# Normed input rows split once, column sums and forget gate in groups of 32 columns, and an opening whose order is written out for all engines

## The chip, the cores and the metric

The kernel runs on one core of one Trainium2 chip. The metric is the device time of one execution in microseconds (us). Engine names are those of the profile: PE (matrix multiply), PEld (its weight loads), DVE (vector), ACT (activation functions), POOL (general purpose), SP (the queue that issues most transfers).

## What is computed

One layer of a trunk over 528 tokens (16 learned ones and 512 of the input), width 1024. The input is normed by the root of the mean of its squares, one large projection gives the features of two branches and their gates, both branches are merged, and a wide MLP follows. Cut to what the change touches:

```python
u = rmsnorm(h, norm_mix[l])                 # u = h * g * rsqrt(mean(h*h) + eps)
proj = u @ w_in[l]
...
f = f + mu * (token_shift(f) - f)
r, k, v, wd, ad, gd = jnp.split(f, ...)
w_log = -jax.nn.softplus(-(w0 + jnp.tanh(wd) @ w_lora_up)) - DECAY_OFFSET
g = jax.nn.sigmoid(gd) @ g_lora_up
...
log_f = jax.nn.log_sigmoid(fl.astype(jnp.float32) + b_f)    # forget gate, 8 heads
F = jnp.cumsum(log_f, axis=1)
```

## The kernel before

All matrices lie with features on the 128 partitions and tokens along the free axis. The 528 tokens are held in two halves of 264 (t = 0 and 1), the 1024 features in eight blocks k of 128 rows, loaded as four chunks c of two blocks each (tiles `xt0` and `xt1`, rows transposed on the host). A product in fp32 accuracy is made of three passes over operands that are split in a high part and a rest, both of type fp32r: high weight with high input, high weight with input rest, weight rest with high input. A split costs ACT a cast (the high part) and DVE a subtraction (the rest). The input's parts are `uhi` and `ulo`, a weight block's are `whi` and `wlo`, made from the loaded `wraw`.

The **opening** works on the two halves one after the other. For each chunk ACT squares it (L352), and PE adds the squares over the partitions with a 128x128 matrix of ones in plain fp32 (L360). At the same time the rows, times the gain of the norm but not yet divided by the root, are split (ACT L355, DVE L356), so that PE can go on at once with the forget gate's eight columns (L365, 24 matmuls of 8 output rows for each half) and with the first weight block, LORA (L304, 24 matmuls for each half). ACT makes the root as an exponential of a logarithm (L368, L369), and DVE multiplies it into the products (L377). The forget gate's logarithm and its running sum follow here (L381 to L387). PE then takes the second weight block, GD, for both halves, while DVE multiplies gain and root into the rows in place (L398) and ACT and DVE split these normed rows a second time (L400, L401). All later projections read this second split.

The results of LORA and GD go through the token shift (`tshift`: ACT L317, DVE L318), a tanh, and another split into `lhi` and `llo` (L270, L271).

After the opening a **planner** sets the order on PE. Streams of work are generators that yield a time at which they can go on; the class `Turns` picks by rank the first stream that is ready by a clock model (`Clock`), whose costs are constants in the code. The streams are: `recurrent` (for each of four pairs of heads: `decay`, `keys`, `rows`, `scores`, `bonus`), `attention`, `fox_features`, `projections` (the weight blocks, L501, 48 matmuls each, which fill PE in between), and later the `chain` streams. The other engines' order is set by the framework's scheduler from priorities. In this kernel the planner's clock starts after the opening (`ck = Clock(nc)` ahead of `turns = Turns(tc, ck)`).

The first pair's work after the opening, in the order in which each step feeds the next: `decay` takes 12 small matmuls `pup` (L733) of `lhi` and `llo`, ACT's tanh (L255) to `sg` and `tha`, a scan on DVE to `lc` (L738), exponentials on ACT to `P` and `lc` (L740, L741). `keys` takes the projected `okk`, squares it (ACT L750), sums per head on PE (`pkk`, L754), takes a logarithm and an exponential on ACT (L757, L758), scales `okk` (DVE L761), and makes `KT` and `BK` on DVE and POOL (L766 to L772). `rows` makes `L` from `okk`, `P` and the second projected block `orr` (DVE L778, L781; ACT L780, L782). `scores` is three times 12 small matmuls `psr` (L807) and three transposes `pbt` (L814), with DVE reading the former out (`Bm`, L808, and `L`, L810). Weight blocks that these steps need are `okk`, `orr` and `ov` (columns `B_PAIR + 3` to `B_PAIR + 5` of the first pair), then the attention's.

All transfers of the opening are issued on SP's queue in program order: parameters, the four chunks of `xt0`, LORA's weights, `xt1`, GD's weights, constants.

## Time and profile before

| | |
|---|---|
| Median of three runs | 848.72 us (846.47 to 850.33) |
| The profiled execution: its own time, its span | 849.18 us, 847.4 us |
| PE busy in the span | 825.8 us (97%) |
| DVE, ACT, POOL busy | 616.5, 454.2, 135.1 us |
| First matmul starts | 4.89 us |
| Last matmul of the opening's two blocks (L304) starts | about 32.0 us |
| Third group of transposes `pbt` starts | 65.14 us |

The profile is of one execution. Its times count from the start of the span, which is 1.8 us shorter than that execution's own time. Engines work at the same time; a busy share says how much of a stretch an engine worked, and the waits say for whom it stood still. Matmuls are pipelined, so one that the profile gives as 0.28 us long is followed by the next after less than half of that; where the text speaks of a step, it means the time from the start of one instruction to the start of the next of a row of equal ones.

### The profile page before, as it was taken

To read this page: it belongs to the slowest core of one execution; us is meant where nothing else is said; L and a number is where in the kernel's file an instruction comes from. 1 tells how busy PE (TensorE), PEld (TensorE's weight loads), DVE (VectorE), ACT (ScalarE), POOL (GpSimd) and SP (SyncE) were. 2 spreads that over 40 slices of the span, in tenths; PEclk is the share of its full clock that TensorE was granted. 3 is DMA by queue.
4 is the path that set the end of the run, shared out by engine and by line. 5 is a ranking of instruction groups with operands and counts; after the bars stand their busy time and mean duration, and the time that the engine had idled before them with its cause. 6 is when DMAs were issued, how large, how long until landed. Compare 5 with 4: busy or idle time off the path is not lost.

```text
span 847.4 us, 15278 instructions
## 1 busy us (share of the span) xinstructions
PE 825.8 (97%) x5740; PEld 678.1 (80%) x5740; DVE 616.5 (73%) x1222; ACT 454.2 (54%) x923; POOL 135.1 (16%) x133
## 2 busy tenths in 40 slices
PE   7889999999999999999999999999999999999998
PEld 6878987878887787677788779888888888888886
DVE  6996996679867965665457564876777677768688
ACT  7767536765656337644555452665355435544452
POOL 1041300004012000000022001203700560055000
PEclk9999999999999999999999999999999999999999
DMA  6231231110222212123486422651743274245421
GB/s 229 58 103 58 72 113 43 45 59 26 77 88 87 75 52 89 51 75 113 138 272 218 154 88 82 201 153 51 248 149 100 85 244 132 86 136 189 119 92 74
DMA packets 51338, 95.88 MB, mean 113 GB/s; under 512 B 5816, under 2 KB 6968, under 8 KB 51264
## 3 DMA queue, kind: packets, MB, share of 16 engines
q1 hardware_dynamic: 47680, 86.52, 32.1%
q0 software_dynamic: 1280, 4.20, 1.6%
q10 hardware_dynamic: 2304, 4.20, 1.5%
q8 instruction: 45, 0.74, 0.4%
q14 instruction: 29, 0.24, 0.1%
HBM read 88.57 MB, written 6.31 MB: 112 GB/s over the span
## 4 chain that ended last, share of the span: by engine, by line
PE 80%; DVE 5%; DMA 4%; ACT 4%; issue 2%; POOL 1%; SPq 0%; ACTq 0%; DVEq 0%; POOLq 0%
PE pj L501 25%; PE po L1150 21%; PE po L1268 12%; PE pd L1268 5%; DMA gl<-gd 2%; PE pw L858 2%; PE po L1120 2%; PE psc L611 1%; DMA wraw<-in_wo 1%; PE py L656 1%; PE ppt L640 1%; PE psr L807 1%; PE pssq L553 1%; PE pch L918 1%; PE pch L924 1%
## 5 line engine op out<-in xcount | busy, mean ns | idle before, releaser
L501 PE MATMUL pj<-uhi,whi 128*128 128x264 f32 (+1 forms) x480 | 165.7, 345 | 0.0
L501 PE MATMUL pj<-ulo,whi 128*128 128x264 f32 (+1 forms) x480 | 154.2, 321 | 1.6 <-DVE ulo L401 1.6
L501 PE MATMUL pj<-uhi,wlo 128*128 128x264 f32 (+1 forms) x480 | 154.0, 321 | 0.0
L501 PEld LDWEIGHTS pj<-uhi,whi 128*128 128x128 f32 x480 | 90.2, 188 | 15.0 <-issue 6.7
L501 PEld LDWEIGHTS pj<-ulo,whi 128*128 128x128 f32 x480 | 90.5, 188 | 8.6 <-DVE ulo L401 2.0
L501 PEld LDWEIGHTS pj<-uhi,wlo 128*128 128x128 f32 x480 | 90.3, 188 | 6.9
L236 DVE TENSOR_TENSOR wlo<-wraw,whi 128x512 fp32r<-128x512 f32 x88 | 68.2, 785 | 37.9 <-ACT whi L235 35.6
L1150 PE MATMUL po<-zhi,whi 128*128 128x512 f32 (+1 forms) x248 | 94.8, 382 | 0.0
L1150 PE MATMUL po<-zlo,whi 128*128 128x512 f32 (+1 forms) x248 | 94.8, 382 | 0.0
L1150 PE MATMUL po<-zhi,wlo 128*128 128x512 f32 (+1 forms) x248 | 94.8, 382 | 0.0
L235 ACT CAST whi<-wraw 128x512 fp32r<-128x512 f32 x88 | 53.7, 616 | 51.5 <-DMA wraw<-in_wup 19.3
L471 DVE TENSOR_TENSOR wlo<-wraw,whi 128x512 fp32r<-128x512 f32 x80 | 61.9, 781 | 17.5 <-ACT whi L470 17.0
L470 ACT CAST whi<-wraw 128x512 fp32r<-128x512 f32 x80 | 49.1, 618 | 43.8 <-PE pj L501 43.2
L270 ACT CAST whi<-t 128x512 fp32r<-128x512 f32 x64 | 39.9, 623 | 44.4 <-DVE wlo L271 20.6
L271 DVE TENSOR_TENSOR wlo<-t,whi 128x512 fp32r<-128x512 f32 x64 | 49.4, 784 | 18.8 <-ACT whi L270 18.0
L1268 PE MATMUL po<-wlo,fhi 128*128 128x512 f32 x160 | 62.7, 392 | 0.2 <-DVE wlo L271 0.2
L1268 PE MATMUL po<-whi,flo 128*128 128x512 f32 x160 | 62.3, 390 | 0.0
L1268 PE MATMUL po<-whi,fhi 128*128 128x512 f32 x160 | 62.0, 389 | 0.0
L1196 POOL TENSOR_TENSOR t<-traw 128x512 f32<-128x512 f32 x24 | 35.3, 1475 | 154.0 <-DVE wlo L271 135.8
L1150 PEld LDWEIGHTS po<-zhi,wlo 128*128 128x128 f32 x248 | 46.6, 188 | 9.0
L1150 PEld LDWEIGHTS po<-zhi,whi 128*128 128x128 f32 x248 | 46.6, 188 | 9.0
L1150 PEld LDWEIGHTS po<-zlo,whi 128*128 128x128 f32 x248 | 46.6, 188 | 9.0
(307 smaller groups left out, 1758.5 us busy)
## 6 DMA issues: line engine op xcount, KB each, us to landing
wraw<-in_win SPq DMA_DIRECT2D x84, 256.0 KB, 2.6
wraw<-in_wup SPq DMA_DIRECT2D x64, 256.0 KB, 3.4
wraw<-in_wdn SPq DMA_DIRECT2D x48, 256.0 KB, 2.6
traw<-in_wdn SPq DMA_DIRECT2D x48, 256.0 KB, 3.1
gd<-gt ACTq DMA_DIRECT2D x16, 256.0 KB, 2.3
wraw<-in_wout SPq DMA_DIRECT2D x16, 256.0 KB, 2.9
gl<-gd SPq DMA_DIRECT2D x16, 256.0 KB, 3.5
wraw<-in_wo SPq DMA_DIRECT2D x16, 256.0 KB, 3.3
```

What stands on the lines that cost most here:

```text
L235: A.copy(hi, raw)
L236: low.tensor_tensor(lo, raw, hi.bitcast(F32), ALU.subtract)
L270: A.copy(hi, x)
L271: V.tensor_tensor(lo, x, hi.bitcast(F32), ALU.subtract)
L470: A.copy(hi, raw)
L471: low.tensor_tensor(lo, raw, hi.bitcast(F32), ALU.subtract)
L501: mm(po, a, b[:, k, a0:a1], start=n == 0, stop=n == 23)
L858: mm(ps_[hs, n - b0, :], lhs(n)[hs], rhs(n)[hs], start=True, stop=True)
L1120: mm(po, a[:, k, 128 * i:128 * i + 128], b[:, k, :], start=n == 0, stop=n == 23)
L1150: mm(po[:, t0:t1], a, b[:, k, t0:t1], start=n == 0, stop=n == 23)
L1196: eng.tensor_tensor(t, sums[c, pair] if c in (T1, T2) else c, d, ALU.add)
L1268: mm(x[i], a[:, k, left, 128 * i:128 * i + 128], c, start=start and k == 0 and n == 0, stop=stop and k == n_pairs - 1 and n == 2)
```

## The change

Both splits of the input become one. The opening is written out in one block, in an order of its own for PE, ACT, DVE and POOL together (`manual_schedule`; before only PE's order was set by hand, and only after the opening).

- **Rows.** The split before the root is gone. For each half the squares are summed first, the root is made, and then chunk by chunk DVE multiplies gain and root into the rows (`scaled`), ACT casts (`upper`), DVE subtracts (`lower`), and PE multiplies LORA and GD together (`products`, 12 matmuls a chunk, 96 in all). The multiplication of the products by the root (L377) is gone.
- **Sums and gate.** The forget gate's matmuls read the rows before the root, in plain fp32, with weights of 32 columns (8 used, the rest zero). Two blocks of a chunk go to two different groups of 32 output rows (`gate`, `group`); chunks 0 and 2 share two groups, 1 and 3 the other two. The second half's sums of squares are made in the same way. Each result is then spread over four groups, which one more fp32 matmul adds up: for the second half's sums with ones after a copy by ACT (`part[0]`), for the gate with a matrix `pick` of 8 columns (`part[1]`, `part[2]`).
- **Weights.** LORA, GD and the first pair's `okk` block are loaded in the opening, the first two ahead of the second half of the input; `okk`'s block is also split there (`primed`).
- **Forget gate.** Its logarithm and running sum move into a function `forget`, called after the first pair's `decay`.
- **Planner.** Its clock now reads the opening (`ck.read()`), and `decay` asks for `lhi` and `llo` to be ready. Weight splits that come later are held behind the opening's last instructions on ACT and DVE (`last`).

```diff
@@ -337,68 +326,144 @@
-            w_lora = load_w(win[B_LORA])
-            for c in range(4):
-                nc.sync.dma_start(xt[1][:, 2 * c:2 * c + 2, :].rearrange("p a b -> p (a b)"), ht[1, c])
-            w_gd = load_w(win[B_GD])
+            raws = []
+            for blk in (B_LORA, B_GD, B_PAIR + 3):
+                if blk == B_PAIR + 3:
+                    for c in range(4):
+                        nc.sync.dma_start(xt[1][:, 2 * c:2 * c + 2, :].rearrange("p a b -> p (a b)"), ht[1, c])
+                for j in range(2):
+                    raw = wp.tile([128, 512], F32, name="wraw", bufs=4)
+                    nc.sync.dma_start(raw, win[blk][:, 512 * j:512 * j + 512])
+                    raws.append(raw)
...
-            rss = []
-            for t in range(2):
-                tk = slice(HT * t, HT * t + HT)
...
+            for hi, lo in primed[B_PAIR + 3]:
+                ohi.append(hi)
+                olo.append(lo)
...
+                sqs[t, c] = sq = xp.tile([128, 2, HT], F32, name="sq", bufs=4)
+                act(sq, xt[t][:, chunks[c], :], AF.Square)
+
+            def group(po, c, k, a, b):
+                g = 2 * (c % 2) + k
+                mm(po[32 * g:32 * g + 32], a, b, start=c < 2, stop=c > 1)
+
+            def gate(t, c):
+                for k in range(2):
+                    group(col[t][1], c, k, wf[:, 2 * c + k, :], xt[t][:, 2 * c + k, :])
+
+            def root(t):
+                act(rss[t], col[t][0], AF.Ln, bias=eps, scale=1.0 / 1024 / (1, 32)[t])
+                act(rss[t], rss[t], AF.Exp, scale=-0.5)
...
+            def scaled(t, c):
+                for k in range(2 * c, 2 * c + 2):
+                    V.scalar_tensor_tensor(xt[t][:, k, :], xt[t][:, k, :], pr[:, C_GN + k:C_GN + k + 1], rss[t], ALU.mult, ALU.mult)
+
+            def upper(t, c):
+                return A.copy(uhi[:, chunks[c], tks[t]], xt[t][:, chunks[c], :])
+
+            def lower(t, c):
+                return V.tensor_tensor(ulo[:, chunks[c], tks[t]], xt[t][:, chunks[c], :], uhi[:, chunks[c], tks[t]].bitcast(F32), ALU.subtract)
+
+            def products(t, c):
+                for q, po in enumerate(pos[t]):
+                    for k in range(2 * c, 2 * c + 2):
+                        i = 2 * q + k // 4
+                        for n, (a, b) in enumerate(passes((ohi[i], olo[i]), U)):
+                            mm(po, a[:, 128 * (k % 4):128 * (k % 4) + 128], b[:, k, tks[t]], start=k + n == 0, stop=k == 7 and n == 2)
...
+            with tc.manual_schedule(engines={ET.PE, ET.Activation, ET.DVE, ET.Pool}):
...
                 for c in range(4):
-                    sq = xp.tile([128, 2, HT], F32, name="sq", bufs=3)
-                    act(sq, xt[t][:, 2 * c:2 * c + 2, :], AF.Square)
-                    for k in range(2 * c, 2 * c + 2):
-                        gn = pr[:, C_GN + k:C_GN + k + 1]
-                        act(uhi[:, k, tk], xt[t][:, k, :], AF.Copy, scale=gn)
-                        V.scalar_tensor_tensor(ulo[:, k, tk], xt[t][:, k, :], gn, uhi[:, k, tk].bitcast(F32), ALU.mult, ALU.subtract)
+                    square(0, c)
+                    for k in range(2):
+                        mm(col[0][0], ones, sqs[0, c][:, k, :], start=c + k == 0, stop=c + k == 4)
+                    if c < 3:
+                        gate(0, c)
+                high(0)
+                rest(0)
+                high(1)
+                rest(1)
+                root(0)
+                gate(0, 3)
+                scaled(0, 0)
+                upper(0, 0)
+                high(2)
+                scaled(0, 1)
+                rest(2)
+                lower(0, 0)
+                high(3)
+                upper(0, 1)
+                for c in range(4):
+                    products(0, c)
+                    square(1, c)
+                    gate(1, c)
+                    for k in range(2):
+                        group(col[1][0], c, k, ones[:, :32], sqs[1, c][:, k, :])
                     if c == 0:
-                        pq = psm("pss")[:, :HT]
-                    for k in range(2):
-                        mm(pq, ones, sq[:, k, :], start=c + k == 0, stop=c + k == 4)
...
-                def normed_shift(po, sl):
-                    V.tensor_tensor(po, po, rss[sl.start // HT], ALU.mult)
-                    shift(po, sl)
-
-                proj(B_LORA, normed_shift, ((tk.start, tk.stop),), w_lora)
-            act(f0, f0, AF.Identity, bias=pr[:8, C_BF:C_BF + 1])
-            V.scalar_tensor_tensor(f1, f0, -1.0, f0, ALU.mult, ALU.max)
-            act(f1, f1, AF.Exp, scale=-1.0)
-            act(f1, f1, AF.Ln, bias=1.0)
-            V.scalar_tensor_tensor(f1, f0, 0.0, f1, ALU.min, ALU.subtract)
-            V.memset(f0, 1.0)
-            V.tensor_tensor_scan(fF, f0, f1, 0.0, ALU.mult, ALU.subtract)
-            nc.sync.dma_start(fF_d, fF)
-            dump("F", fF)
-            act(lf[:64], lf[:64], AF.Tanh)
+                        rest(3)
+                    if c == 2:
+                        high(4)
+                    if c < 2:
+                        scaled(0, c + 2)
+                        upper(0, c + 2)
+                    if c < 3:
+                        lower(0, c + 1)
+                rest(4)
+                A.copy(part[0], col[1][0])
+                col[1][0] = psm("pss")[:, :HT]
+                mm(col[1][0], ones, part[0], start=True, stop=True)
+                root(1)
+                tanh(tiny, eps)
+                scaled(1, 0)
+                upper(1, 0)
+                shifts[0](pos[0][0], tks[0])
+                scaled(1, 1)
+                lower(1, 0)
+                upper(1, 1)
+                shifts[1](pos[0][1], tks[0])
+                high(5)
+                for c in range(4):
+                    products(1, c)
+                    if c < 2:
+                        A.copy(part[1 + c], col[c][1])
+                        scaled(1, c + 2)
+                        last["ACT"] = upper(1, c + 2)
+                    if c < 3:
+                        lower(1, c + 1)
+                    if c == 1:
+                        rest(5)
+                last["DVE"] = shifts[0](pos[1][0], tks[1])
+                V.tensor_reduce(pick, ident.rearrange("p (g a) -> p a g", g=4)[:, :8, :], AX.X, ALU.add)
+                for t in range(2):
+                    pf = psm("pf")[:8, :HT]
+                    mm(pf, pick, part[1 + t], start=True, stop=True)
+                    V.tensor_tensor(f0[:, tks[t]], pf, rss[t][:8], ALU.mult)
+                shifts[1](pos[1][1], tks[1])
+            tanh(lf[:64], lf[:64])
...
-            shift = tshift(12 + B_GD, lfs[1])
-            proj(B_GD, normed_shift, w=w_gd)
-            for t in range(2):
-                tk = slice(HT * t, HT * t + HT)
-                for c in range(4):
-                    for k in range(2 * c, 2 * c + 2):
-                        V.scalar_tensor_tensor(xt[t][:, k, :], xt[t][:, k, :], pr[:, C_GN + k:C_GN + k + 1], rss[t], ALU.mult, ALU.mult)
-                    kk = slice(2 * c, 2 * c + 2)
-                    A.copy(uhi[:, kk, tk], xt[t][:, kk, :])
-                    V.tensor_tensor(ulo[:, kk, tk], xt[t][:, kk, :], uhi[:, kk, tk].bitcast(F32), ALU.subtract)
...
-        ck = Clock(nc)
+        ck.read()
...
-        converted = []
-
         def convert(job, raws):
-            low = V
-            converted.append(job)
+            if job[2] in primed:
+                return job, primed.pop(job[2])
             w = []
             for raw in raws:
                 hi = wp.tile([128, 512], F32R, name="whi", bufs=4)
                 lo = wp.tile([128, 512], F32R, name="wlo", bufs=4)
-                A.copy(hi, raw)
-                low.tensor_tensor(lo, raw, hi.bitcast(F32), ALU.subtract)
+                after(A.copy(hi, raw), last["ACT"])
+                after(V.tensor_tensor(lo, raw, hi.bitcast(F32), ALU.subtract), last["DVE"])
                 w.append((hi, lo))
...
+        forgot = Event()
+
+        def forget():
+
+            s_ = act(f0, f0, AF.Identity, bias=pr[:8, C_BF:C_BF + 1])
+            V.scalar_tensor_tensor(f1, f0, -1.0, f0, ALU.mult, ALU.max)
+            pin = pinned(s_)
+            after(act(f1, f1, AF.Exp, scale=-1.0), pin)
+            after(act(f1, f1, AF.Ln, bias=1.0), pin)
+            V.scalar_tensor_tensor(f1, f0, 0.0, f1, ALU.min, ALU.subtract)
+            V.memset(f0, 1.0)
+            V.tensor_tensor_scan(fF, f0, f1, 0.0, ALU.mult, ALU.subtract)
+            nc.sync.dma_start(fF_d, fF)
+            forgot.done = True
...
-                    yield lambda: max(ck.ready(*lw), banks(2))
+                    yield lambda: max(ck.ready(lhi, llo, *lw), banks(2))
...
+            forget()
```

How instructions stand now is shown at three places. In the names, `xt_116` and `xt_117` are the two halves before, `xt_117` and `xt_118` now; `pss` is a sum of squares, `pf` the forget gate, `pj` a product with a weight block. Rows of the changed kernel carry its own line numbers: L402 and L365 are its sums and groups, L390 `products`, L437 the matmul that adds up `part[0]`, L566 the later projections.

The first place is PE at the end of the statistics of the second half. Before, between LORA's first and second half:

```order
L304 MATMUL pj<-uhi,wlo 128x264
L360 MATMUL pss<-sq,ones 128x264 x8
L365 MATMUL pf<-uhi,wf_152 8x264
L365 MATMUL pf<-ulo,wf_152 8x264
L365 MATMUL pf<-uhi,wf_153 8x264
```

Now, behind the last chunk of the first half:

```order
L390 MATMUL pj<-uhi,olo_148 128x264
L365 MATMUL pf<-xt_118,wf 32x264 x2
L365 MATMUL pss<-sq,ones 32x264 x2
L437 MATMUL pss<-part_159,ones 128x264
L390 MATMUL pj<-uhi,ohi_141 128x264
L566 MATMUL pj<-uhi,whi 128x264
L566 MATMUL pj<-ulo,whi 128x264
L566 MATMUL pj<-uhi,wlo 128x264
...
L390 MATMUL pj<-ulo,ohi_141 128x264
```

Behind L437 stands one matmul of the second half's products, then 12 of `okk`'s block on the first half's rows, then the rest of the products.

The second place is ACT around the root of the second half. Before:

```order
L352 ACTIVATE sq<-xt_117 128x528
L355 ACTIVATE uhi<-xt_117,pr 128x264
L368 ACTIVATE rs<-pss,eps 128x264
L369 ACTIVATE rs<-rs 128x264
L381 ACTIVATE f_107<-f_107,pr 8x528
L470 CAST whi<-wraw 128x512
```

Now (L372 and L373 are the root, `tiny` a tanh of one column, `tm` the token shift):

```order
L435 COPY part_159<-pss 128x264
L372 ACTIVATE rs<-pss,eps 128x264
L373 ACTIVATE rs<-rs 128x264
L255 ACT_TABLE_LOAD
L255 ACTIVATE tiny<-eps 128x1
L380 CAST uhi<-xt_118 128x2x264
L303 ACTIVATE tm<-pj,pr 128x264
```

The split (L355 before, L380 now) stands behind the root, and the load of the tanh table between the two.

The third place is DVE in the first pair's `keys` and `rows`. Before:

```order
L755 TENSOR_SCALAR sq<-pkk 128x264 x2
L314 MEMSET tm 128x1
L318 SCALAR_TENSOR_TENSOR orr<-pj,pr_65,tm 128x264
L471 TENSOR_TENSOR wlo<-wraw,whi 128x512
L761 SCALAR_TENSOR_TENSOR okk<-okk,pr,sq 128x528
L778 SCALAR_TENSOR_TENSOR L_705<-okk,P 128x9x63
```

Now:

```order
L843 SCALAR_TENSOR_TENSOR okk<-okk,pr,sq 128x528
L599 SCALAR_TENSOR_TENSOR f_109<-f_108,f_109 8x528
L860 SCALAR_TENSOR_TENSOR L_655<-okk,P 128x9x63
L861 TENSOR_SCALAR L_655<-okk 128x9
L848 SCALAR_TENSOR_TENSOR KT<-okk,lc 128x9x64
L600 MEMSET f_108 8x528
L849 SCALAR_TENSOR_TENSOR BK<-tha,KT 128x9x64
L601 SCALAR_TENSOR_TENSOR fF<-f_108,f_109 8x528
L304 SCALAR_TENSOR_TENSOR orr<-pj,pr_65,tm 128x264 x2
L536 TENSOR_TENSOR wlo<-wraw,whi 128x512
L863 TENSOR_TENSOR L_655<-orr,P 128x9x64
```

Three steps of `forget` (L599, L600, L601) now stand among these, and both halves of `orr`'s token shift come behind them.

73 lines of the change are left out of this document (37 added, 36 removed).

## The prediction, on record before the result was known

> **What bounds the kernel now.** I read the page's first lines, then the stretches of the opening, then what PE waits for. In the stretches the columns are length, busy time (and instructions) of PE, PEld, DVE, ACT and POOL, granted clock, transfer share, GB/s.
>
> ```profile
> span 847.4 us, 15278 instructions
> PE 825.8 (97%) x5740; PEld 678.1 (80%) x5740; DVE 616.5 (73%) x1222; ACT 454.2 (54%) x923; POOL 135.1 (16%) x133
> ...
> 4.89:10.05 5.16, 5.16 (x13) 4.01 (x13) 3.87 (x8) 5.16 (x12) 0.00 (x0) 1.00 1.03 377
> 10.05:34.30 24.25, 23.39 (x178) 20.42 (x175) 22.33 (x52) 18.93 (x39) 0.28 (x2) 1.00 0.32 109
> 34.30:56.70 22.40, 20.13 (x153) 18.96 (x151) 19.62 (x36) 17.29 (x35) 6.02 (x7) 1.00 0.31 93
> 56.70:65.40 8.70, 7.20 (x93) 5.06 (x93) 8.44 (x15) 2.19 (x5) 3.69 (x4) 1.00 0.35 113
> 65.40:120.00 54.60, 54.15 (x417) 47.84 (x416) 45.21 (x92) 31.78 (x61) 10.23 (x10) 1.00 0.21 66
> ```
>
> PE is the bound from its first matmul on. Between 10.05 and 34.3 us, where the change works, it stands still for 0.9 us only. So a gain needs less PE work or fewer waits, and a new wait on PE is paid in full. Behind 65 us PE is again busy to 99%, and there the order of the changed kernel is that of before on every engine; so what PE has lost or won by then should stay to the end. All of PE's waits in this part:
>
> ```profile
> PE pj L501 <- DVE ulo L401: 1.6, 2, 1.3
> PE pkk L754 <- ACT sq L750: 0.7, 1, 0.7
> PE psr L807 <- DVE Bm L808: 0.6, 1, 0.6
> PE pup L733 <- DVE llo L271: 0.6, 1, 0.6
> PE pbt L814 <- POOL KT L772: 0.5, 1, 0.5
> PE pbt L814 <- DVE L L810: 0.4, 1, 0.4
> PE pup L733 <- ACT lhi L270: 0.3, 1, 0.3
> ```
>
> They add to 4.7 us. That is the most that better order could win here.
>
> **PE's clock.** The granted clock reads 1.00 throughout, but the durations tell more. An fp32 sum is recorded as two matmuls; here are twelve such halves of the first sums and sixteen of the later ones (PE and PEld alone):
>
> ```profile
> 4.89:9.90 5.01, 5.01 (x12) 3.87 (x12) 1.00 1.03 377
> 16.88:20.24 3.36, 3.36 (x16) 2.85 (x16) 1.00 0.40 137
> ```
>
> 0.42 us a half against 0.21: until about 10 us PE runs at half pace. A whole sum costs 0.84 us there and 0.42 later.
>
> **Prices.** FP32R matmuls of 264 columns (72 of L304); a pair of fp32 matmuls in two column halves (L656, 512 columns, up to L939 in the same tile shape); a change of tile shape (L501 to L807):
>
> ```profile
> 23.42:32.20 8.78, 8.78 (x72) 8.66 (x71) 1.00 0.21 62
> ...
> 180.25 1.08 PE L656 MATMUL py<-pT,vt 128*64 128x512 f32 x4
> 181.16 0.40 PE L939 MATMUL pch<-uv,bkT 128*64 128x64 f32 x8
> ...
> 56.41 0.40 PE L501 MATMUL pj<-uhi,wlo 128*128 128x512 f32 x1
> 56.73 0.89 PE L807 MATMUL psr<-L,BK 64*64 64x128 f32 x24
> ```
>
> An FP32R matmul steps in 8.78/72 = 0.122 us. The two 512-column matmuls took 0.91 us; one alone would take 512/264 x 0.42 = 0.81, so the halves run side by side. No row shows groups of 32 columns: side by side a pair costs 0.91 x 264/512 = 0.47, one after the other 0.84. I take 0.47, the nearest row. The shape change cost 0.32 - 0.23 (the step of the 512-column matmul) = 0.09, say 0.1; it may be 0 to 0.2.
>
> **PE's work.** Removed: 48 gate matmuls, 5.9 us, and eight sums of the second half, 3.4: together 9.3. Added: 12 pairs (four for the first half's gate, eight for the second half), 5.6; one sum 0.4; two matmuls with `pick`, 0.8; about 16 shape changes, 1.6: together 8.4. The 96 products stay. So PE wins only 0.9 us.
>
> **The walk.** The rest is order, so I went through it engine by engine with these steps (L368, L369: root; L398: rows scaled; L400, L401: split; L390: table load; L235, L236: weight split):
>
> ```profile
> 12.01 0.48 ACT L368 ACTIVATE rs<-pss,eps 128x264 f32<-128x264 f32 x1 [0.75 <-PE pss L360]
> 12.80 0.41 ACT L369 ACTIVATE rs<-rs 128x264 f32<-128x264 f32 x1
> ...
> 19.71 4.13 DVE L398 SCALAR_TENSOR_TENSOR xt<-xt,pr,rs 128x264 f32<-128x264 f32 x10
> 27.99 1.68 ACT L400 CAST uhi<-xt 128x528 fp32r<-128x528 f32 x3
> 30.96 1.91 DVE L401 TENSOR_TENSOR ulo<-xt,uhi 128x528 fp32r<-128x528 f32 x3
> 29.69 1.28 ACT L390 ACT_TABLE_LOAD   x1
> 7.84 1.12 ACT L235 CAST whi<-wraw 128x512 fp32r<-128x512 f32 x2
> 14.53 0.67 DVE L236 TENSOR_TENSOR wlo<-wraw,whi 128x512 fp32r<-128x512 f32 x1
> ```
>
> 1. *First half's statistics.* PE starts at 4.89 as before. Eight sums and three pairs stand ahead of the root: 5.4 us at full pace with the shape changes. Until 10.05 PE does 2.6 of it, the rest takes to 13.1. Before, the root started at 12.01.
> 2. *First gap.* Root 0.9, two rows scaled 0.9, cast 0.6; one product can start at 15.8. The second waits for the rest of the input, and on DVE the two rows of the next chunk and a weight's rest stand ahead of it, the latter behind ACT's cast: first `ulo` at 17.6. Apart from one pair and one matmul PE stands still from 13.6 to 17.6: 3.8 us. Before, the unscaled split was ready, and PE never waited for the root.
> 3. *First half's products.* 48 matmuls, 5.9 us, and four times two pairs with two shape changes, 4.6: PE is the bound, to 27.9.
> 4. *Second gap.* ACT's copy, a sum, the root, the table load with `tiny` 1.5, the cast 0.6: the next product starts at 32.2. PE has one sum of 0.4 in this time and waits 3.9. `okk`'s twelve matmuls can't fill it, since they stand behind that product.
> 5. *Second half's products.* DVE and ACT hand over to each other, the token shifts between; PE waits 1.6 more (first `ulo`s of two chunks) and ends the 96 products at 41.4, with 14 of `okk`'s matmuls done. Before, the 72 later products of L304 ended at 32.2, and by 41.4 the `pup` and some 47 of L501 were done.
> 6. *Into the first pair.* With 0.4 us for `pick`, PE is through `okk`, `orr`, `ov`, `pup` and `pkk` at 60.4. But LORA's second half, on which `decay` waits, comes out 15 us later than before. ACT and DVE now do `decay`, `keys` and `forget` together:
>
> ```profile
> 44.85 0.49 DVE L318 SCALAR_TENSOR_TENSOR okk<-pj,pr,tm 128x264 f32<-128x264 f32 x1
> 49.98 0.76 DVE L761 SCALAR_TENSOR_TENSOR okk<-okk,pr,sq 128x528 f32<-128x528 f32 x1
> ...
> 27.86 0.69 DVE L385 SCALAR_TENSOR_TENSOR f<-f,f 8x528 f32<-8x528 f32 x1
> 29.01 0.50 DVE L386 MEMSET f<- 8x528 f32 x1
> 29.79 1.23 DVE L387 TENSOR_TENSOR_SCAN fF<-f,f 8x528 f32<-8x528 f32 x1
> ...
> 61.33 0.55 DVE L808 TENSOR_TENSOR Bm<-psr,cs 128x384 f32<-128x384 f32 x1
> ...
> 65.45 0.48 PE L501 MATMUL pj<-uhi,whi 128*128 128x512 f32 x1
> ```
>
> Before it took 5.1 us from `okk`'s second half to `okk` scaled. Now `okk` comes at 47.9, and ACT has the rest of `decay`, a table load and two steps of `forget` in between: scaled at 55.7. Then DVE does three steps of `forget` (2.4 us) ahead of `orr` and the next weight's rest, which ends at 62.2. PE, free at 60.4, waits 1.8 for it. `Bm` comes at 66.6 instead of 61.33, and PE waits 0.9 twice more. The matmul that before started at 65.45, behind the third `pbt`, starts at 71.9: **6.4 us later**.
>
> As a check: PE's waits are now 3.8 + 3.9 + 1.6 + 0.4 + 1.8 + 1.8 = 13.3 us against 4.7, less 0.9 of work: 7.7. The walk gives 6.4, since before had short pauses that the waits leave out (its first six gate matmuls filled 9.96 to 10.92, 0.2 more than their work); I keep the walk. Bounds: groups one after the other, +5.2 (12 times 0.37, those at half pace twice); as well packed as to hide half of each pair, -2.1; shape changes, 1.6 either way; DVE's weight rests in the tail slower or faster beside POOL, 1.1 either way. The profiled execution took 849.18, 0.46 above the median: 849.18 + 6.4 = 855.6 for such an execution, 855.1 against the median. I add 0.4 for part of the clock rival below: **855.5 us**.
>
> **Rivals.**
>
> *The clock falls back in a gap.* At the end of the program:
>
> ```profile
> 843.07 0.39 PE L1268 MATMUL po<-whi,flo 128*128 128x512 f32 x1
> ...
> 842.80:846.20 3.40, 0.66 (x3) 0.19 (x2) 1.37 (x2) 0.00 (x0) 0.00 (x0) 1.00 0.60 233
> 846.30:847.40 1.10, 0.00 (x0) 0.00 (x0) 0.00 (x0) 0.00 (x0) 0.00 (x0) 0.51 0.00 0
> ```
>
> About 3 us after the last matmul the granted clock is half. Both gaps are that long. It took PE up to 5.2 us to get out of half pace at the start; in half that time a fall costs 1.3 us, at worst 2.6. Time: 857. Against it: each gap holds a matmul or two. [...]
>
> *The groups run one after the other*, so that the change does not do what its groups are for. Every pair costs 0.84: 855.1 + 5.2 = 860.5. For it: no row with 32 columns; against it: L656.
>
> *The tail absorbs it.* If PE's 4.5 us of waits in step 6 shrink to the 1.5 of before, because the scheduled steps of ACT and DVE are shorter than I took them, the time is 852, which is within 0.5%.
>
> *DVE's relief decides: faster.* DVE is full while PE makes the opening:
>
> ```profile
> 15.00:20.00 5.00, 5.00 (x32) 4.54 (x32) 5.00 (x14) 4.26 (x11) 0.00 (x0) 1.00 0.36 118
> ```
>
> The change takes 16 subtractions of about 0.45 and four products by the root off DVE, nearly 9 us. If that shortens the hand-over of chunks until PE waits less than 1 us after each root, the 3.2 us that PE waited for `ulo`, `llo`, `lhi` and `sq` go: 845.5. Against it: each root stands on one chain of dependent steps, which a free DVE does not shorten.
>
> **Chances.** Forecast 0.52; clock 0.17; groups in turn 0.08; tail absorbs 0.16; DVE's relief 0.07. About 0.5%, 4.2 us, is what a measurement can tell from no change: the three runs before lie 3.9 us apart. A small part of the forecast's own spread lies inside that bound: slower 0.73, within 0.20, faster 0.07. Range 851 to 861 us: it leaves out the faster case and the ends of the last.
>
> **What would show it.** Each step has a place in the new profile: the second root's start (L372) near 29 us; PE idle of 3 us or more ahead of the first `ulo` product and behind L437; L390's last matmul near 41; `okk` scaled (L843) near 55.7; PE's wait ahead of the 512-column matmuls; the matmul behind the third `pbt` near 72. Pairs in L365 stepping in 0.47 or 0.84 decide the groups, the granted clock in the gaps the clock rival. I am wrong if PE is idle less than 2 us in the two gaps together, or if the third `pbt` comes before 67 us.

## The result, and the profile after

The changed kernel takes 859.98 us (median of four executions, 858.18 to 861.47), the kernel before 849.53 in the same comparison: 1.0131 times as long, with an interval of 1.0113 to 1.0148. That is 10.4 us slower. Slower was forecast: 855.5 us, made of 6.4 us of the walk and 0.4 for the clock rival on top of 848.72. The measured time lies inside the range, near its upper end. The profiled execution took 861.47 us, with a span of 859.7.

The page's head of the changed kernel:

```profile
span 859.7 us, 15219 instructions
PE 832.0 (97%) x5730; PEld 677.1 (79%) x5730; DVE 608.5 (71%) x1204; ACT 449.3 (52%) x910; POOL 134.6 (16%) x133
```

PE's waits up to 78 us (time in all, times, longest):

```profile
PE pj L390 <- ACT uhi L380: 5.1, 2, 3.1
PE pss L402 <- ACT sq L361: 5.0, 1, 5.0
PE pj L566 <- DVE orr L304: 1.5, 1, 1.5
PE pj L390 <- DVE ulo L383: 1.3, 1, 1.3
PE pj L566 <- DVE wlo L536: 1.3, 1, 1.3
PE pj L566 <- DVE lf L304: 0.5, 1, 0.5
PE pss L437 <- ACT part L435: 0.5, 1, 0.5
```

Without the wait for the first input (L402), PE now waits 10.2 us in this part, against 4.7 before. PE is busy 6.2 us more, though it has ten matmuls less. The next view, cut into stretches of 3.41 us, says why. The columns are length, busy time (and instructions) of PE, PEld, DVE, ACT and POOL, granted clock, transfer share and GB/s.

```profile
12.13:15.54 3.41, 1.35 (x9) 0.48 (x7) 1.67 (x4) 1.65 (x4) 0.00 (x0) 1.00 0.65 237
15.54:18.95 3.41, 2.11 (x8) 1.81 (x9) 3.00 (x7) 2.22 (x5) 0.00 (x0) 0.50 0.29 79
18.95:22.36 3.41, 3.41 (x16) 1.82 (x15) 2.98 (x6) 3.17 (x6) 0.00 (x0) 0.50 0.27 75
22.36:25.78 3.42, 3.42 (x27) 2.64 (x27) 0.21 (x1) 0.04 (x1) 0.00 (x0) 1.00 0.20 77
29.19:32.60 3.41, 1.75 (x11) 0.62 (x10) 0.18 (x1) 1.48 (x4) 0.00 (x0) 1.00 0.00 0
32.60:36.02 3.42, 1.02 (x6) 0.82 (x7) 1.90 (x5) 2.19 (x4) 0.00 (x0) 1.00 0.00 0
36.02:39.43 3.41, 3.41 (x17) 3.41 (x17) 2.94 (x7) 2.68 (x6) 0.00 (x0) 0.50 0.00 0
39.43:42.84 3.41, 3.41 (x29) 3.41 (x29) 2.56 (x6) 1.92 (x5) 0.00 (x0) 1.00 0.11 33
63.33:66.74 3.41, 1.11 (x6) 0.49 (x4) 3.41 (x5) 1.25 (x3) 3.02 (x3) 1.00 0.03 5
66.74:70.15 3.41, 2.95 (x7) 2.16 (x7) 3.41 (x7) 0.78 (x2) 3.33 (x2) 0.50 0.57 141
```

PE's clock falls to half three times here, always behind a stretch in which PE stood still for most of the time, and it comes back only behind a stretch in which PE was busy for 2.95 us or more. The three falls last 6.8, 3.4 and 3.4 us: whole multiples of 3.41 us, on one grid. The matmuls of the timeline show the two paces:

```profile
15.48 0.56 PE L390 MATMUL pj<-uhi,ohi 128*128 128x264 f32 x1 [2.06 <-ACT uhi L380]
17.35 0.59 PE L390 MATMUL pj<-ulo,ohi 128*128 128x264 f32 x1 [1.30 <-DVE ulo L383]
17.73 0.42 PE L390 MATMUL pj<-uhi,olo 128*128 128x264 f32 x1
17.95 0.42 PE L390 MATMUL pj<-uhi,ohi 128*128 128x264 f32 x1
...
23.82 0.64 PE L365 MATMUL pf<-xt,wf 128*32 128x264 f32 x4
24.29 0.62 PE L365 MATMUL pss<-sq,ones 128*32 128x264 f32 x4
24.84 0.39 PE L390 MATMUL pj<-uhi,ohi 128*128 128x264 f32 x1
...
34.48 0.39 PE L390 MATMUL pj<-uhi,ohi 128*128 128x264 f32 x1 [3.06 <-ACT uhi L380]
...
75.53 0.48 PE L566 MATMUL pj<-uhi,whi 128*128 128x512 f32 x1
```

At half pace a product steps in 0.22 us instead of 0.12. The last row is the matmul behind the third `pbt`; before it started at 65.45, so the change has lost **10.1 us** there. The lateness then stays: the first `pssq` of the fox branch comes 10.05 us late (85.69), the fifth 10.03 (231.78). At 285 us the clock of this execution falls once more (behind 1.4 us of waits, 0.9 and 0.6, that the kernel before has too, without a fall) and adds 1.6. So the place behind the third `pbt` measures a change of the opening apart from what happens later, and I give it for every run below.

| start, us | before | after | predicted |
|---|---|---|---|
| First root (L368, now L372) | 12.01 | 12.90 | 13.1 |
| First product; first with `ulo` | – | 15.48; 17.35 | 15.8; 17.6 |
| Second root | 20.64 | 31.45 | about 29 |
| Product behind the second root | – | 34.48 | 32.2 |
| Last of the 96 products | – | 44.32 | 41.4 (its end) |
| `okk` scaled | 49.98 | 58.81 | 55.7 |
| First 512-column matmul | 55.95 | 65.20 | 60.4, and a wait of 1.8 |
| Matmul behind the third `pbt` | 65.45 | 75.53 | 71.9 |

### The profile page after: what moved, and what is told of

The parts are those of the page before. It is cut to its first block, busy times and chain, and to the rows that moved or that the text cites. A ratio compares the mean times of both kernels' runs of the same rounds, so it can differ in the third digit from the quotient of the medians.

```text
span 859.7 us, 15219 instructions
## 1 busy us (share of the span) xinstructions
PE 832.0 (97%) x5730; PEld 677.1 (79%) x5730; DVE 608.5 (71%) x1204; ACT 449.3 (52%) x910; POOL 134.6 (16%) x133
## 4 chain that ended last, share of the span: by engine, by line
PE 83%; DMA 5%; ACT 5%; DVE 5%; issue 2%; SPq 0%; POOL 0%; ACTq 0%; DVEq 0%; POOLq 0%
PE pj L566 26%; PE po L1233 20%; PE po L1351 12%; PE pd L1351 5%; DMA gl<-gd 2%; PE pj L390 2%; PE pw L940 2%; PE po L1203 2%; PE psc L692 1%; DMA wraw<-in_wup 1%; PE psr L889 1%; PE py L737 1%; PE ppt L721 1%; PE pssq L633 1%; PE pch L1000 1%
## 5 line engine op out<-in xcount | busy, mean ns | idle before, releaser
L566 PE MATMUL pj<-uhi,whi 128*128 128x264 f32 (+1 forms) x480 | 166.7, 347 | 2.0 <-DVE orr L304 1.5
L566 PE MATMUL pj<-uhi,wlo 128*128 128x264 f32 (+1 forms) x480 | 155.4, 324 | 1.3 <-DVE wlo L536 1.3
L566 PE MATMUL pj<-ulo,whi 128*128 128x264 f32 (+1 forms) x480 | 155.0, 323 | 0.0
L566 PEld LDWEIGHTS pj<-uhi,whi 128*128 128x128 f32 x480 | 90.9, 189 | 17.4 <-issue 8.3
L566 PEld LDWEIGHTS pj<-uhi,wlo 128*128 128x128 f32 x480 | 91.2, 190 | 9.2 <-DVE wlo L536 1.7
L566 PEld LDWEIGHTS pj<-ulo,whi 128*128 128x128 f32 x480 | 91.1, 190 | 6.7 <-issue 1.7
L236 DVE TENSOR_TENSOR wlo<-wraw,whi 128x512 fp32r<-128x512 f32 x84 | 67.0, 808 | 39.7 <-ACT whi L235 37.3
L235 ACT CAST whi<-wraw 128x512 fp32r<-128x512 f32 x84 | 51.3, 617 | 52.9 <-DMA wraw<-in_wup 22.6
L535 ACT CAST whi<-wraw 128x512 fp32r<-128x512 f32 x78 | 47.8, 618 | 44.4 <-PE pj L566 44.0
L536 DVE TENSOR_TENSOR wlo<-wraw,whi 128x512 fp32r<-128x512 f32 x78 | 59.4, 769 | 16.5 <-ACT whi L535 16.2
```

The lines of the kernel that those rows point to most:

```text
L235: A.copy(hi, raw)
L236: low.tensor_tensor(lo, raw, hi.bitcast(F32), ALU.subtract)
L535: after(A.copy(hi, raw), last["ACT"])
L536: after(V.tensor_tensor(lo, raw, hi.bitcast(F32), ALU.subtract), last["DVE"])
L566: mm(po, a, b[:, k, a0:a1], start=n == 0, stop=n == 23)
```

## The experiments

The lateness is that of the matmul behind the third `pbt` against 65.45 us, from the one profiled execution; the ratio is to the kernel before, with its interval. The lateness has a scatter of its own: seven of these runs have the same instructions ahead of the first root, and it starts between 12.58 us (`whole_sums`) and 13.76 us (`no_tiny`). So a difference of about 1 us in this column says little by itself.

| run | median us | ratio | lateness us |
|---|---|---|---|
| the change | 859.98 | 1.0131 (1.0113 to 1.0148) | 10.1 |
| `warm_gaps` | 859.51 | 1.0120 (1.0101 to 1.0140) | 8.3 |
| `warm_all` | 858.16 | 1.0103 (1.0079 to 1.0126) | 7.2 |
| `early_groups` | 853.95 | 1.0055 (1.0039 to 1.0072) | 5.2 |
| `gates_late` | 856.43 | 1.0087 (1.0072 to 1.0103) | 7.2 |
| `no_tiny` | 863.78 | 1.0167 (1.0146 to 1.0187) | 15.2 |
| `forget_late` | 861.23 | 1.0139 (1.0120 to 1.0158) | 13.6 |
| `whole_sums` | 860.86 | 1.0132 (1.0113 to 1.0151) | 10.3 |
| `order2` | 851.36 | 1.0026 (1.0012 to 1.0040) | 3.0 |
| `order4` | 850.32 | 1.0011 (0.9997 to 1.0024) | 2.2 |
| `order5` | 848.02 | 0.9965 (0.9952 to 0.9978) | -2.3 |
| `inopen` | 852.14 | 1.0014 (1.0001 to 1.0027) | 2.6 |
| `order5_warm` | 849.94 | 0.9994 (0.9977 to 1.0010) | -2.2 |

**What the clock costs.** Two runs fill PE's gaps with matmuls whose result nobody reads. They take away nothing that PE's products wait for.

```diff
+            def fill(n):
+                for _ in range(n):
+                    mm(pos[1][1][:, :128], ones, ones, start=True, stop=True)
...
                             mm(po, a[:, 128 * (k % 4):128 * (k % 4) + 128], b[:, k, tks[t]], ...)
+                            if t + c + q + k + n == 0:
+                                fill(5)
...
                 gate(0, 3)
+                fill(7)
...
                 mm(col[1][0], ones, part[0], start=True, stop=True)
+                fill(9)
```

> The changed kernel with 21 matmuls that compute nothing, put on PE into its two gaps: 7 behind the last gate pair of the first half, 5 behind the first product, 9 behind the one sum of the second half. They write a bank that is free there, so no wait is taken away. Theory A (the gaps let PE's clock fall, and the half pace costs as much as the waits): the two stretches of half clock at 15.5 to 22.4 and 36.0 to 39.4 us are gone, PE's waits move by little, and the time is about 4 us less (2.4 for the 4.9 us in which PE worked at half pace in the first stretch, 1.6 for the 3.3 us of the second): 856. Theory B (the waits alone set the end, ACT and DVE hand over no faster): the clock reads 1.00 and the time stays at 860.

Both falls are gone (10 to 20 and 28 to 42 us read 1.00), and the first 512-column matmul starts at 62.05 instead of 65.20: 3.15 us earlier, three quarters of what theory A gave. But at the end of the opening the clock now falls for two grid steps instead of one (63.2 to 70.0 us), and the lead shrinks to 1.8 us. In the median only 0.5 us is left, less than the runs differ, so by its number A missed. The second run fills that last gap too:

```diff
                             for a, b in passes(wk(w, k), U):
+                                if a1 - a0 > 300 and n in (0, 2) and len(filled) < 2:
+                                    filled.append(psm("fl")[:, :128])
+                                    for _ in range((6, 5)[n // 2]):
+                                        mm(filled[-1], ident, ident, start=True, stop=True)
                                 mm(po, a, b[:, k, a0:a1], start=n == 0, stop=n == 23)
```

> The changed kernel with matmuls that compute nothing in all its three gaps: the 21 of the run with two filled gaps, and at the end of the opening six ahead of the first 512-column matmul and five behind its second, where PE waits for `orr` and a weight's rest; with them the first `psr` comes six 512-column matmuls earlier in PE's order. With two gaps filled the opening was 3.1 us ahead at the first 512-column matmul, and 1.3 of it was lost again in a fall of the clock over two windows. Theory A (the clock's falls are worth what they slow): no stretch of half clock before 75 us, 1.3 us less than with two gaps filled, 858 or less. Theory B (in the last part DVE sets the pace, the half clock there is hidden): the clock stays up and the time stays at 859.5.

The stretch from 62 to 72.5 us, first of the run with two gaps filled, then of this one:

```profile
62.00:72.50 10.50, 9.16 (x69) 6.32 (x69) 9.86 (x15) 3.56 (x7) 5.44 (x5) 0.67 0.52 153
```

```profile
62.00:72.50 10.50, 9.45 (x105) 7.02 (x106) 10.41 (x18) 3.51 (x7) 5.46 (x5) 1.00 0.54 163
```

The clock stays up and the lateness falls by another 1.1 us. The median is 1.35 us below that of the run with two gaps filled, about what A gave, but the two intervals overlap; against the change it is 1.8 us, and those overlap too. So the whole times do not prove the price, and it rests on the three profiled executions, whose first roots start within 0.04 us (12.86 to 12.90). The second run also moves the first `psr` six matmuls ahead, so its 1.1 us is not the clock's alone. With no fall in the opening the change is still 7.2 us late. By these traces **2.9 us of its 10.1 are the clock, and 7.2 are waits and work**. The half clock stretches PE's matmuls by more than that: by half of 5.0 us (17.35 to 22.36), of 3.4 and of 2.95, 5.7 us in all. The first two falls, 4.2 of it, cost 3.15 us at the first 512-column matmul; the last one costs nothing that shows: from that matmul to the one behind the third `pbt` it is 10.33 us in the change, 10.55 here, and 10.34 in `order5` below, at a clock of 1.00.

**The second gap.** The second half's groups and its root are moved ahead of the first half's last products.

```diff
                 for c in range(4):
                     products(0, c)
-                    square(1, c)
-                    gate(1, c)
-                    for k in range(2):
-                        group(col[1][0], c, k, ones[:, :32], sqs[1, c][:, k, :])
+                    for c2 in ((0, 1), (2, 3), (), ())[c]:
+                        square(1, c2)
+                        gate(1, c2)
+                        for k in range(2):
+                            group(col[1][0], c2, k, ones[:, :32], sqs[1, c2][:, k, :])
...
+                    if c == 1:
+                        A.copy(part[0], col[1][0])
+                    if c == 2:
+                        col[1][0] = psm("pss")[:, :HT]
+                        mm(col[1][0], ones, part[0], start=True, stop=True)
+                        root(1)
```

> The changed kernel with the second half's squares, gate groups and sum groups moved ahead: those of chunks 0 and 1 stand behind the first chunk's products, those of chunks 2 and 3 behind the second's, then the copy of the partial sums, and the one sum and the root behind the third's. So the second root's chain runs while PE makes the last products of the first half. Theory A (the second gap costs its wait of 3.5 us and the half clock behind it 1.6): both are gone, 855. Theory B (the second half's hand-over from DVE and ACT, not the root, sets the first `ulo`): PE waits for `ulo` instead, and the time falls by less than 1.5: 859.

The lateness falls by 4.9 us and the median by 6 us against the change: theory A by the time. The clock no longer falls behind this gap (this execution reads 0.996 in the mean, the change's 0.989), but the gap is not gone: of the wait for the first cast behind the second root 1.59 us is left. And some 2 us of the gain is not the gap. The groups of two chunks now stand together, and they cost as much as those of one did, twice in place of four times:

```profile
24.18 0.67 PE L365 MATMUL pf<-xt,wf 128*32 128x264 f32 x8
24.65 0.64 PE L365 MATMUL pss<-sq,ones 128*32 128x264 f32 x8
25.22 0.39 PE L390 MATMUL pj<-uhi,ohi 128*128 128x264 f32 x1
```

Sixteen halves take 1.04 us, where the change's eight took 1.02 (23.82 to 24.84 above). The two blocks of a chunk go to two of the four groups of output rows, the next chunk's to the other two; all four together took no longer than two.

**The first gap.** The first half's gate pairs move behind its sums.

```diff
-                    if c < 3:
-                        gate(0, c)
...
                 root(0)
-                gate(0, 3)
+                for c in range(4):
+                    gate(0, c)
```

> The changed kernel with the first half's gate groups behind its eight sums instead of among them. The sums then end near 10.2 us (3.7 us at half pace make 4.4 of them, the rest 1.5 us), the root starts 2.6 us earlier, and the four pairs fill part of the first gap. Theory A (PE's half pace at the start and the gap cost what the trace shows): -2.6 for the root, and the first fall of the clock is gone, -2.4: 855. Theory B (the first products wait for something else, the weights or DVE's order, once the root is early): 858 or more.

```profile
4.60 6.08 PE L402 MATMUL pss<-sq,ones 128*128 128x264 f32 x16 [4.60 <-ACT sq L361]
10.61 1.10 PE L365 MATMUL pf<-xt,wf 128*32 128x264 f32 x16
13.31 0.39 PE L390 MATMUL pj<-uhi,ohi 128*128 128x264 f32 x1 [1.60 <-ACT uhi L380]
```

The root starts at 10.72, 2.2 us earlier, and the lateness falls by 2.9 us, the median by 3.6. The other 2 us of A did not come, since the clock still falls behind the gap, for one step of the grid in place of two (0.991 in the mean against 0.989; a step at half clock is 0.002 of the span). The reason is the second row: all four pairs, sixteen halves, are done in 1.10 us. One after the other they would take 16 times 0.21, 3.36, as an estimate from the halves of the kernel before. They are too short to fill the gap.

**The table load.** The one-column tanh ahead of the second half's first cast is left out.

```diff
                 root(1)
-                tanh(tiny, eps)
```

> The changed kernel without the one-column tanh that loads ACT's table ahead of the second half's first cast; the load then stands ahead of LORA's tanh. Theory A (the load lies on the second root's chain): the gap is 1.5 us shorter, and the clock may not fall behind it, another 1.6: 857 to 858.5. Theory B (the load is paid again later, on LORA's chain into the first pair): 860.

3.8 us slower than the change, 5.1 later at the third `pbt` (0.9 of it already at the first root). The product behind the second root comes 2.58 us after it instead of 3.03: 0.45 us sooner, not 1.5, since DVE's scaling of the rows (0.90) had run beside the load. And behind the opening ACT and DVE now work in another order; `okk`'s second half reaches ACT's square only at 60.47, at the end of a chain that the change has done by 52.6:

```profile
PE pkk L835 <- ACT sq L831: 4.7, 1, 4.7
```

The load does come back on LORA's chain, as B has it: it stands on ACT from 46.92 us for 1.28, right ahead of LORA's tanh. What it costs there this run cannot tell, beside a wait of 4.7 us and a clock that falls for two steps in each of three gaps (0.987 in the mean). It shows that a step taken out ahead of the planner changes what it does behind.

**The forget gate.** Its steps are called behind the first pair's `rows`.

```diff
             yield from pairs[0].decay()
-            forget()
...
                     q.rows()
+                    if j == 0 and g == 0:
+                        forget()
```

> The changed kernel with the forget gate's steps called behind the first pair's `rows` instead of behind its `decay`, so that `orr` and the next weight's rest stand ahead of them on DVE. In the changed kernel PE waits 1.5 us for `orr` and 1.3 for the weight's rest there. Theory A (the three steps of forget, 2.4 us on DVE, are what PE waits for at the end of the opening): both waits go and the time falls by 2 to 3 us: 857.5. Theory B (the way over `Bm`, two more products of DVE's queue, sets the pairs' pace, and PE's wait only moves to `psr` or `pbt`): 859.5 to 860.

Theory B. PE's waits for `orr` and the weight are gone, and others have come, on POOL and on `Bm`:

```profile
PE pbt L896 <- POOL KT L854: 2.5, 1, 2.5
...
PE psr L889 <- DVE Bm L890: 1.1, 1, 1.1
```

At the third `pbt` it is 3.5 us later than the change. Forget's three steps now stand on DVE between 66.0 and 72.5 us, ahead of `Bm` (73.38), and the first of them takes 2.62 us, beside a product of POOL (64.68 to 68.09), where it took 0.69; behind these waits, and behind the second gap, the clock falls for two steps where it fell for one (0.988 in the mean). The ratio is that of the change within its interval. So moving forget later only moves the waits; the run `inopen` below has DVE's products beside POOL's again.

**The groups.** The second half's sums are made as before, with 128 columns.

```diff
-                        group(col[1][0], c, k, ones[:, :32], sqs[1, c][:, k, :])
+                        mm(col[1][0], ones, sqs[1, c][:, k, :], start=c + k == 0, stop=c + k == 4)
...
-                A.copy(part[0], col[1][0])
-                col[1][0] = psm("pss")[:, :HT]
-                mm(col[1][0], ones, part[0], start=True, stop=True)
```

> The changed kernel with the second half's sums as before, with 128 columns of ones and one accumulator; the copy of the partial sums and the sum over them are left out. Only the gate stays in groups of 32 columns. Theory A (a pair of groups that stands alone costs 0.47 to 0.55 us, nearly what it replaces, and the copy and the last sum stand on the second root's chain): PE does 4 x 0.3 = 1.2 us more and 0.4 less, the gap is 1.1 us shorter: the time stays within 1 us of 860. Theory B (the groups are the change's gain and their removal costs the full 3.4 - 2.2 us or more): 861.5 or more.

Lateness 10.3 against 10.1, ratio 1.0132 against 1.0131: theory A. In the order of the change, the sums in groups of 32 columns win nothing. Whether they win something once they stand together, no run shows.

**A better order.** Four runs build one up. The first joins the two moved pieces and lets DVE make the first `ulo` ahead of the next chunk's rows:

```diff
                 high(2)
+                lower(0, 0)
                 scaled(0, 1)
                 rest(2)
-                lower(0, 0)
```

> The changed kernel with three pieces of order: the gate pairs of the first half behind its sums (measured alone: 2.9 us earlier at the third `pbt`), the second half's groups and root early (4.9 us earlier), and on DVE the first `ulo` ahead of the next rows and weight rest, 1.3 us earlier. Theory A (each shortens its own gap, so they add): 10.1 - 2.9 - 4.9 - 1.3 = 1 us behind the kernel before: 850. Theory B (they shorten the same gap or the end of the opening gives it back): two of the three at best, 852 to 854.

The lateness is 3.0 us, 2.0 more than A's sum; the clock falls at 27.4 us for one step and at 58.1 for two (26 to 31 us read 0.66, 58 to 65 read 0.51). The next run adds nine matmuls of ones from 1.5 us on, sets all of the second half's groups behind the first chunk's products, and the root and the load behind the second's:

```diff
+                for _ in range(9):
+                    mm(pos[1][1][:, :128], ones, ones, start=True, stop=True)
...
-                    for c2 in ((0, 1), (2, 3), (), ())[c]:
+                    for c2 in ((0, 1, 2, 3), (), (), ())[c]:
```

> The run before this one (three pieces of order), and two more: nine matmuls of ones that compute nothing, on PE from 1.5 us on, while the first input is under way, so that its clock is up for the first sums; and all four of the second half's groups behind the first chunk's products, the root and the table load behind the second's. Theory A (the half pace at the start delays the first root by 2 us, and the second gap's last 1.6 us goes): 3 to 4 us less than the run with three pieces. Theory B (the first root waits for the input's transfers, not for PE): the root starts no earlier than 10.5 us, and only the second gap's 1.6 is won.

Only 1 us, no more than the scatter of the starts. The root starts at 10.4, but the product behind the second root waits 2.3 us: DVE has the rest of a weight (L357) ahead of the rows, and that weight's cast stands on ACT behind root and table load.

```profile
24.24 0.69 DVE L357 TENSOR_TENSOR wlo<-wraw,whi 128x512 fp32r<-128x512 f32 x1 [3.30 <-ACT whi L354]
24.85 0.89 DVE L377 SCALAR_TENSOR_TENSOR xt<-xt,pr,rs 128x264 f32<-128x264 f32 x2
```

So the third run moves this cast and rest ahead of the root:

```diff
-                    if c == 2:
+                    if c == 1:
                         high(4)
+                        rest(4)
...
-                rest(4)
```

> The run with nine early matmuls and the early root (850.3 us, PE waits 2.3 us for the second half's first cast), with one weight's cast and rest moved from behind that root to ahead of it; the order on PE stays. In that run DVE waited for this cast until 24.2 us and only then scaled the second half's first rows. Theory A (the cast stands on the root's chain): the first rows are scaled 1.1 us earlier, and the time is about 1 us less: 849.3. Theory B (the end of the opening, bound by DVE behind `okk`, gives it back): 850.3.

```profile
9.00:40.00 31.00, 26.88 (x224) 22.53 (x223) 24.10 (x51) 22.74 (x46) 0.28 (x2) 1.00 0.38 127
52.00:63.00 11.00, 8.21 (x95) 5.66 (x96) 10.91 (x18) 3.51 (x7) 6.16 (x5) 1.00 0.48 153
```

The lateness falls by 4.5 us to -2.3, four times what A gave. The second gap is gone, and the clock does not fall in the opening of this execution. Some of that belongs to this execution: 1.1 us of it stands already at the first root (9.27 against 10.40), with the same instructions ahead, and waits of 1.6 us in the first gap and of 1.5 and 1.3 in the last are still there, and in the timed executions the mean clock lies between 0.994 and 1.000. At 0.9965 (0.9952 to 0.9978) this version is faster than both kernels, but only 0.35% below the kernel before. Last, the forget gate is written into the opening, where DVE had 2.4 us idle:

```diff
+                        for t in range(2):
+                            A.copy(part[1 + t], col[t][1])
+                        V.tensor_reduce(pick, ...)
                         root(1)
-                        tanh(tiny, eps)
...
                 scaled(1, 0)
                 upper(1, 0)
+                for t in range(2):
+                    pf = psm("pf")[:8, :HT]
+                    mm(pf, pick, part[1 + t], start=True, stop=True)
+                    V.tensor_tensor(f0[:, tks[t]], pf, rss[t][:8], ALU.mult)
+                act(f0, f0, AF.Identity, bias=pr[:8, C_BF:C_BF + 1])
...
+                            act(f1, f1, AF.Ln, bias=1.0)
+                            tanh(tiny, eps)
...
+                V.tensor_tensor_scan(fF, f0, f1, 0.0, ALU.mult, ALU.subtract)
                 last["DVE"] = shifts[0](pos[1][0], tks[1])
```

> The run with the moved weight, and the whole forget gate written into the opening: its two matmuls stand in the second gap, its Exp and Ln ahead of the tanh table load (which moves off the root's chain too), its scan on DVE behind the last `ulo`, where DVE had 2.4 us idle. Theory A (the three steps of forget on DVE, 2.4 us, and its four on ACT are what PE waits for in front of the first pair, 2.8 us): both waits fall to under 1 us, the second gap is 1 us shorter, and the time is 3 us less: 846 to 847, below the kernel before. Theory B (DVE's weight rests and products beside POOL set the pace of the pairs whatever stands ahead): 849 or more.

Theory B. PE no longer waits for `orr`, but 2.2 us for the weight's rest and 1.9 for `lf`, ahead of which the scan now stands. DVE in this run:

```profile
48.76 2.02 DVE L866 SCALAR_TENSOR_TENSOR L<-okk,P 128x567 f32<-128x567 f32 x1
50.70 1.14 DVE L867 TENSOR_SCALAR L<-okk 128x9 f32<-128x9 f32 x1
...
54.09 2.40 DVE L550 TENSOR_TENSOR wlo<-wraw,whi 128x512 fp32r<-128x512 f32 x1
```

and POOL:

```profile
48.74 1.43 POOL L856 TENSOR_TENSOR BK<-sg,lc 128x576 f32<-128x576 f32 x1 [6.96 <-ACT lc L829]
50.25 1.56 POOL L860 TENSOR_TENSOR KT<-BK,P 64x576 f32<-64x576 f32 x1
...
53.82 2.12 POOL L858 TENSOR_TENSOR KT<-BK,P 64x1152 f32<-64x1152 f32 x1
```

In the change the same two products of DVE took 0.73 and 0.16 us, while POOL was idle (59.76 to 62.46 us). The weight's rest at this place took 1.75 in the change too, also beside POOL (L852, 63.78 to 66.59), and 1.75 in `order5`; with POOL idle one took 0.68 in the change (45.75). Here L866 runs beside a product of POOL and ends 0.61 us behind it (50.78 and 50.17), L550 0.55 (56.49 and 55.94), and L867 0.03 (51.84 and 51.81). What made them longer is not shown; the rows give only how long they took side by side. With less to do DVE comes to these products just when POOL does (48.76 and 48.74), and L866 and L867 together took 2.3 us longer than in the change: about the 2.4 us that were taken off DVE.

So by these rows nothing is won, but they do not give the whole 4.9 us by which this run is later than `order5`. Its clock falls twice in the opening, at 13.35 us for one step and at 57.7 for two, and that of `order5` never (the views above read 1.00). From the first 512-column matmul to the one behind the third `pbt`, first here, then in `order5`:

```profile
53.68:68.05 14.37, 10.86 (x99) 7.51 (x97) 12.46 (x19) 4.32 (x9) 5.65 (x6) 0.76 0.33 97
```

```profile
52.77:63.11 10.34, 8.32 (x96) 5.74 (x97) 10.25 (x18) 3.51 (x7) 5.39 (x5) 1.00 0.52 164
```

It takes 4.0 us longer; PE stands still 1.5 us longer and works 2.5 us longer on the same matmuls, half of which now run at half pace. The timed executions fit: the mean clock lies between 0.992 and 0.996 here and between 0.994 and 1.000 there. A run of this order with the clock kept up was not made, so the share of each is an estimate from these two traces.

The last run fills what is left of the gaps in the best order:

> The best order so far (848.0 us, 0.35% below the kernel before) with matmuls that compute nothing in what is left of its gaps: four behind the first half's gate pairs, and the eleven at the end of the opening. Its clock read 0.994 to 1.000 in seven executions. Theory A (its slower executions are those in which the clock falls in a gap): the clock reads 0.997 or more in all, and the time is 1 us less, 847. Theory B (the spread comes from elsewhere, or DVE hides it): 848 and the same spread.

Theory B: no gain, 0.9994 (0.9977 to 1.0010), and a clock of 0.996 or 0.997 in seven of its twelve executions. In the profiled one the opening is as good (-2.2 us) and clean of falls; the 2.1 us by which its span is longer come at 494 us, in a wait in front of the MLP that all these kernels have, here of 2.0 us instead of 1.1, with a fall behind it (stretches of 2 us):

```profile
494.00:496.00 2.00, 0.36 (x3) 0.37 (x4) 1.17 (x2) 0.73 (x4) 0.00 (x0) 1.00 0.31 107
496.00:498.00 2.00, 2.00 (x10) 1.77 (x9) 0.93 (x2) 1.16 (x2) 0.00 (x0) 0.60 0.00 0
498.00:500.00 2.00, 2.00 (x6) 1.54 (x5) 0.69 (x1) 0.02 (x1) 0.00 (x0) 0.55 0.00 0
```

At least this part of the spread is a fall of the clock far behind the opening. That the fillers themselves cost something is not shown.

## Why the prediction was right or wrong

The sign was right and so was the mechanism: two gaps behind the two roots, and work of LORA that comes too late for the first pair. The size was 6.4 us where 10.1 were lost.

*First half's statistics, first gap.* Predicted 13.1, 15.8 and 17.6; measured 12.90, 15.48 and 17.35. Waits 3.8 predicted, 2.06 + 1.30 = 3.4 measured.

*First half's products.* This is the step that failed. I had PE through them at 27.9 and the second root at about 29; it came at 31.45. The price of a pair was right at full pace (0.47 us, 23.82 to 24.29). But from 15.54 to 22.36 PE ran at half pace, and eleven products and the two pairs behind them took 4.6 us (17.35 to 21.97) instead of about 2.4.

*Second gap.* From the second root to the next product I had 3.2 us; 3.03 were measured. PE waited 0.48 + 3.06 + 0.52 = 4.1, with 3.9 predicted. Then the clock fell again, and the last product ended at 44.6, 3.2 us after the predicted 41.4; 2.3 of it had been lost by the product behind the root. The 1.6 us of waits for `ulo` that I had put there did not come: at half pace PE was slower than DVE.

*Into the first pair.* From `okk` scaled to the matmul behind the third `pbt` I had 16.2 us, 16.7 were measured (15.5 before). I had PE wait 1.8 for the weight's rest and 0.9 twice for `Bm`; it waited 1.47 for `orr`, 1.29 for the rest, and not for `Bm`, since it was slow again (in `early_groups`, without the fall, it waited 0.7 for it).

*The rival that should have been in the sum* is the clock's. I gave it 0.17 and 857, put 0.4 us of it into the forecast, and argued that each gap holds a matmul or two, which would keep the clock up. The stretches 12.13:15.54 and 32.60:36.02 above disprove this: PE was busy 1.35 and 1.02 us of 3.41, and the clock fell all the same. It fell in every gap, and again in the last one, where I had not looked for it. No run shows the 0.4: in all four executions of the change the mean clock lies below that of the profile before, at 0.988 to 0.994 against 0.999, and filled gaps price the falls at 2.9 us; with it 6.4 becomes 9.3, and the missing 0.8 is PE's work and waits, within the bounds given. That the time still fell inside the range is owed to the width of the range, not to a priced clock. I had taken it that the clock falls only where PE has no matmul at all, as at the end of the program, for some 3 us; here it fell behind gaps whose longest single waits were 2.06 and 3.06 us.

*Two sums do not come out of their own terms.* 10.05 and the 2.8 us that were left make 12.85 for the first root, not 13.1 (12.90 was measured); and half of twelve pairs of 0.47 is 2.8, not the 2.1 of the bounds. Neither changes the forecast by more than 0.3 us.

*The other rivals.* Groups in turn: disproved by 0.47. The tail absorbs it, and DVE's relief: neither came. DVE was idle for 9.85 us ahead of the rows that it scales behind the second root, and PE waited all the same for the chain of dependent steps, as was argued:

```profile
32.42 0.90 DVE L377 SCALAR_TENSOR_TENSOR xt<-xt,pr,rs 128x264 f32<-128x264 f32 x2 [9.85 <-ACT rs L373]
```

*What would have shown it wrong* did not happen: PE was idle 7 us in the two gaps, and the third `pbt` came at 75.23.

## What to carry to other kernels

A wait of PE has two prices, the wait and the half pace behind it: where a stretch of 3.41 us will have PE busy for 1.4 us or less, as ahead of three of the four falls in the change (1.35, 1.02 and 1.11 us; the fourth came behind 1.96), add the second to the sum. The cure is PE work that depends on nothing late, left for the time in which a root is made (`early_groups`), and no step of another chain in that root's queue (`order5`). Matmuls of 32 columns belong together in fours in one place of the order, not as one pair per chunk.

## What was not expected of the hardware

- Four groups of 32 columns in fp32: sixteen halves of 264 columns in 1.04 to 1.10 us, against 3.36 at 0.21 each, about three times as fast. Two groups: eight halves in 1.02. Four rounds of 0.21 (a half in the trace before), each with as many groups as differ, and 0.2 for the two changes of shape (one cost 0.09 in the trace before) give 1.04 for both, as an estimate.
- The clock counts more than gaps. In the change it fell behind stretches with PE busy 1.35, 1.02 and 1.11 us of 3.41, and not behind one with 1.75 (29.19 to 32.60). It did not rise behind 2.11 us at half pace. Near 285 us it fell behind 1.96 us (281.78 to 285.19), more than the 1.75 behind which it had stayed up, and later it stayed up behind 1.84 (428.55 to 431.96). So busy time alone does not tell the falls from the rest in this trace, and what counts stays open.
- A fall can be free. In the change the last fall of the opening cost nothing that shows: from the first 512-column matmul to the one behind the third `pbt` it took 10.33 us with it, and 10.34 in `order5` without any. A fall of two steps, in `warm_gaps`, cost 1.3.
